# Every second up-projection weight pair: low part by an accumulating transfer instead of a VectorE subtraction

## The chip, the cores and the metric

The kernel runs on one core of one Trainium2 chip. The metric is the device time of one execution in microseconds (us). The time before is 1998.34 us, the median of two runs (1998.25 and 1998.43).

## The reference

One step of a hybrid encoder layer for 384 token rows (256 prompt frames and 8 streams of 16 frames), all in float32, with `D_MODEL` = 2048 and `D_FF` = 5632:

- `p = rmsnorm(x) @ w_in`, a convolution branch and an attention branch, and `x = x + (gate_a * a_out + gate_b * b_out) @ w_out` (the mixer);
- `up = rmsnorm(x) @ w_up`, with `w_up` of 2048 x 11264; the first 5632 columns go through a causal convolution of 3 taps and SiLU, the others multiply the result;
- `x = x + (silu(conv(g_half)) * u_half) @ w_down`, with `w_down` of 5632 x 2048.

The new keys, values, forget logits and convolution states are outputs as well. The change touches only how the weight tiles of `w_up` get ready for the matrix products.

## The kernel before, in words

**Three products for one.** The matmuls work on a rounded float32 format (`F32R`). To keep float32 accuracy, each operand is kept as a pair: `hi`, the rounded value, and `lo`, the rounded difference to the full value. A product is then three matmuls: activation hi by weight hi (line 251), activation hi by weight lo (L252), activation lo by weight hi (L253).

**Weight pairs.** Weights are streamed from memory once. The unit is a "pair": two blocks of 128 rows by 512 columns, one tile of 128 x 2 x 512 float32 (512 KB). The list `plan` holds all pairs in the order in which the products use them. `fetch` (L135 to L142) issues the load of one pair from SyncE's DMA queue (SP) into a tile `raw` (L140). `split_rows` makes `hi` by a ScalarE copy (L149) and `lo` by a VectorE subtraction `raw - hi` (L150). `raw`, `hi` and `lo` have three buffers each. So the `hi` and `lo` of pair n+3 can only be written when TensorE has finished with pair n, and the `raw` of pair n+3 can only be loaded when the last reader of `raw` of pair n has finished.

**Order.** `gemm` takes one pair for two steps of k. Before each pair it calls `ahead(3)`, which fetches and splits until three pairs are ready. The order of TensorE's instructions is that of the program (a manual schedule). Those of the other engines are placed by a scheduler when the program is built, with a priority for the splits (`SPLIT_AHEAD`); on the chip each engine works through its list strictly in order. The same holds for the DMA issues of SP and GpSimd (POOL).

**The feed-forward part.** `w_up` is used in 11 groups (g = 0 to 10) of 512 gate columns and 512 other columns. A group is two jobs of 8 pairs each: first the gate half, then the other half. Each pair feeds 18 matmuls (2 k steps, 3 token tiles, 3 products). After some groups the matching part of `w_down` is multiplied: the order is up 0 to 3, down, up 4 to 6, down, up 7 and 8, down, up 9 and 10, down.

**What else runs on the engines in a group.** At the end of each job ScalarE takes the three results out of PSUM (`up_evac`, L1003, tile `tok`). `turn` transposes them: three VectorE transposes into `tb` (L274), and 16 small SP transfers `uT<-tb` (L278). Behind the gate half, ScalarE copies the turned tile into `extf` (L1012), POOL fills in the borders (`L1018`, `L1019`) and copies the state out (`lc`, L1032), VectorE works the three taps (`gc`, L1027 and L1029), and ScalarE takes the SiLU (`sg`, L1031). Behind the other half, VectorE multiplies (L1058), ScalarE and VectorE split the product into hi and lo (`act`, L1060 and L1061).

Of the kernel before, what the change touches and what calls it, by code (L numbers as in the profile page):

```python
# [10 lines left out]
AF = mybir.ActivationFunctionType  # L11
ALU = mybir.AluOpType
# [29 lines left out]
def hybrid_step(  # L42
# [9 lines left out]
    nc = tc.nc  # L52
# [24 lines left out]
    def f(ap):  # L77
        return ap.bitcast(F32)
# [14 lines left out]
    def queued(d, chain=True):  # L93
        e = d.ins.engine
        if chain and e in newest:
            tc.add_manual_dep(d.ins, newest[e], mybir.DependencyInfo(
                mybir.DependencyClass.NoSync, mybir.DependencyReason.DATA), reason="queue")
        newest[e] = d.ins.name

    def load_x(c, n):  # L100
        cs = slice(c * P, (c + n) * P)
        o = c % 4 * P
        queued(nc.sync.dma_start(xs[c // 4][:, 0:2, o:o + n * P],
                                 x_prompt[0, :, cs].rearrange("(t p) d -> p t d", p=P)))
        queued(nc.sync.dma_start(xs[c // 4][:, 2, o:o + n * P], xin[2][:, cs]))
# [22 lines left out]
    def stream_tile():  # L128
        return rp.tile([P, 2, 512], F32, tag="raw", bufs=3, name="raw")
# [5 lines left out]
    def fetch(srcs):  # L135
        raw = stream_tile()
        o = 0
        for s in srcs:
            n = s.shape[-1]
            queued(nc.sync.dma_start(raw[:, :, o:o + n], s), len(plan) >= v_last)  # L140
            o += n
        return raw, o  # L142

    def split_tiles():
        return [wp.tile([P, 2, 512], F32R, tag=tag, bufs=3, name=tag) for tag in ("hi", "lo")]

    def split_rows(hi, lo, raw, o, k):
        first = in_first()
        queued(nc.scalar.copy(hi[:, k, :o], raw[:, k, :o]), first)  # L149
        queued(tt(lo[:, k, :o], raw[:, k, :o], f(hi[:, k, :o]), op=ALU.subtract), first)  # L150

    def split(raw, o):
        hi, lo = split_tiles()
        split_rows(hi, lo, raw, o, slice(0, 2))
        return hi, lo

    plan = []

    def planned(w, k0, cols, nk, *more):
        for k in range(k0, k0 + nk, 2):  # L160
            for cl in (cols,) + more:
                plan.append([w[0, k * P:(k + 2) * P, c:c + n].rearrange("(k p) n -> p k n", p=P) for c, n in cl])
# [11 lines left out]
    FFN_PLAN = [("up", g) for g in range(4)] + [("down", (0, 1, 2))]  # L174
# [12 lines left out]
    for what, g in FFN_PLAN:  # L187
# [3 lines left out]
        else:  # L191
            for cols in N_COLS:
                planned(w_down, 4 * g[0], cols, 4 * len(g))

    v_last = len(plan) - 16

    def in_first():
        return len(plan) >= v_last - 4
    ready = []
# [6 lines left out]
    def ahead(n):  # L206
        while plan and len(ready) < n:
            with tc.high_priority(offset=SPLIT_AHEAD):
                if x_left and (len(plan) - v_last) in range(3, 14, 2):
                    load_x(x_left.pop(0), 2)  # L210
                ready.append(split(*fetch(plan.pop(0))))

    def grouped(tiles):
        def get(k):
# [13 lines left out]
    def gemm(jobs, sides=(), wide=False):  # L228
        for js in jobs:
# [4 lines left out]
            for j, k in [(j, k + i) for k in range(0, js[0]["nk"], 2) for j in js for i in range(2)]:  # L234
                nb, n, nk, ps = len(j["ps"]), j["n"], j["nk"], j["ps"]
                kk = k % 2
                if kk == 0:
                    ahead(2 if len(plan) > v_last + 3 else 3)
                    hi, lo = ready.pop(0)
                ah, al = j["act"](k)  # L240
                st, sp = k == 0, k == nk - 1
                for m in range(nb):
                    s = slice(m * P, (m + 1) * P)
                    if j["kind"] == "A":
                        o = ps[m][:, :NT]
                        mm(o, hi[:, kk, s], ah, start=st, stop=False)  # L246
                        mm(o, hi[:, kk, s], al, start=False, stop=False)  # L247
                        mm(o, lo[:, kk, s], ah, start=False, stop=sp)  # L248
                    else:
                        o = ps[m][:, :n]  # L250
                        mm(o, ah[:, s], hi[:, kk, :n], start=st, stop=False)  # L251
                        mm(o, ah[:, s], lo[:, kk, :n], start=False, stop=False)  # L252
                        mm(o, al[:, s], hi[:, kk, :n], start=False, stop=sp)  # L253
                if sp:
                    with tc.high_priority(offset=EVAC_AHEAD):
                        for m in range(nb):
                            j["evac"](m, ps[m])
                    if "post" in j:
                        j["post"]()
                    if "done" in j:  # L260
                        j["done"]()
                tick(sides)
# [51 lines left out]
    with tc.manual_schedule(engines={ENG.SP, ENG.Activation, ENG.DVE}):  # L314
        nc.vector.memset(junk[:, 0:1], 0.0)
        nc.scalar.dma_start(gm_row[:], norm_mix_g[0].rearrange("(c p) -> c p", p=P))
        nc.scalar.activation(junk[:, 1:2], junk[:, 0:1], AF.Identity)
        load_x(0, 1)
        first = stream_tile()
        fetch_row(first, plan[0], 0)  # L320
        load_x(1, 1)
        fetch_row(first, plan.pop(0), 1)
        second = fetch(plan.pop(0))
        load_x(2, 2)
        warm = misc_tile()

        def warm_up(n):
            for _ in range(n):
                mm(warm[:, :P], ident[:], ident[:], start=True, stop=True)

        warm_up(WARM)
        pv = misc_tile()
        tr(pv[:, :16], gm_row[:], ident[:16, :16])
        nc.vector.tensor_copy(gm[:], pv[:, :16])
        hi, lo = split_tiles()
        split_rows(hi, lo, first, V_COLS[0][0][1], slice(0, 1))
        x_chunk(0)
        warm_up(FILL)
        split_rows(hi, lo, first, V_COLS[0][0][1], slice(1, 2))
        x_chunk(1)  # L340
        ready.append((hi, lo))
        ready.append(split(*second))
# [461 lines left out]
    for h in range(H):  # L804
        hi, lo = aHL[h // 4][:, 0, h % 4, :], aHL[h // 4][:, 1, h % 4, :]
# [326 lines left out]
```

## Time and profile before

| what | value |
|---|---|
| median of the runs shown | 1998.34 us |
| the profiled execution, its own time | 1997.35 us |
| its span (first to last instruction) | 1995.5 us |
| granted clock of TensorE in it | 0.999 |
| busy: TensorE / weight loads | 1986.3 / 1677.0 us |
| busy: VectorE / ScalarE / GpSimd | 1158.3 / 771.0 / 88.8 us |
| moved by DMA | 292.54 MB |

The profile comes from one profiled execution. Busy time is the time in which an engine's instructions ran; idle time has the instruction that ended it beside it, where the profile can tell. "L149" is line 149 of the kernel before. In the changed kernel the lines behind 151 stand 6 to 14 lines lower. In the timeline, each row has the start, the duration, the engine, the line and the operation; in brackets stands how long the engine had been idle and who ended that. SPq is SyncE's queue of DMA issues.

### The profile page before, as it was taken

The page shows a single profiled execution, that of the slowest core. Times are in us where ns is not written, and L with a number is a line of the kernel's source. Part 1 is how long each engine was busy: PE and PEld are TensorE (multiplying, and loading weights), DVE is VectorE, ACT ScalarE, POOL GpSimd, SP SyncE. Part 2 cuts the span into 40 slices and gives each one's busy share as a digit, 9 for nine tenths or more (in the row PEclk, how much of TensorE's full clock was granted, in tenths as well). Part 3 has the DMA queues.
Part 4 walks back from the last instruction along what each step waited for, and adds up shares of the span by engine and source line. Part 5 has one row for each costly group of instructions (what it writes and reads, how often), then busy time and mean ns, then how long its engine had stood idle before and what let it go on. Part 6 is the DMA issues. An engine that isn't in the chain of part 4 may idle for free.

```text
span 1995.5 us, 24829 instructions
## 1 busy us (share of the span) xinstructions
PE 1986.3 (100%) x9383; PEld 1677.0 (84%) x9383; DVE 1158.3 (58%) x1635; ACT 771.0 (39%) x1209; POOL 88.8 (4%) x216
## 2 busy tenths in 40 slices
PE   9999999999999999999999999999999999999999
PEld 9888999888888888888888888888888888888887
DVE  4455888888755487676455453345453345534563
ACT  5535454433334433344444442244342234323421
POOL 1000011000000000000100000000000000000000
PEclk9999999999999999999999999999999999999999
DMA  6564767444443435534555554445454445445543
GB/s 192 148 183 116 220 150 162 145 135 131 131 135 118 132 122 171 161 119 137 153 153 156 148 157 135 130 140 165 139 168 132 132 139 164 144 132 152 154 158 106
DMA packets 225384, 292.54 MB, mean 147 GB/s; under 512 B 61254, under 2 KB 112857, under 8 KB 225257
## 3 DMA queue, kind: packets, MB, share of 16 engines
q1 hardware_dynamic: 224945, 290.38, 49.7%
q8 instruction: 73, 1.20, 0.3%
q0 software_dynamic: 288, 0.57, 0.2%
q14 instruction: 46, 0.38, 0.1%
q10 hardware_dynamic: 32, 0.01, 0.0%
HBM read 266.98 MB, written 7.86 MB: 138 GB/s over the span
## 4 chain that ended last, share of the span: by engine, by line
PE 97%; DVE 2%; DMA 0%; issue 0%; SPq 0%; ACT 0%; DVEq 0%; ACTq 0%
PE acc L251 20%; PE acc L253 20%; PE acc L252 20%; PE misc L253 10%; PE misc L251 10%; PE misc L252 10%; PE acc L246 2%; PE acc L247 2%; PE acc L248 2%; DVE lo L150 0%; DVE mixT L268 0%; DMA bs<-c_dr 0%; PE misc L305 0%; PE misc L642 0%; PE misc L675 0%
## 5 line engine op out<-in xcount | busy, mean ns | idle before, releaser
L150 DVE TENSOR_TENSOR lo<-raw,hi 128x1024 fp32r<-128x1024 f32 (+2 forms) x481 | 580.3, 1207 | 676.3 <-ACT hi L149 674.1
L149 ACT CAST hi<-raw 128x1024 fp32r<-128x1024 f32 (+2 forms) x481 | 496.1, 1031 | 966.5 <-PE misc L253 781.1
L251 PE MATMUL acc<-hi,xg 128*128 128x512 f32 x704 | 275.1, 391 | 0.0
L253 PE MATMUL acc<-hi,xg 128*128 128x512 f32 x704 | 274.1, 389 | 0.0
L252 PE MATMUL acc<-lo,xg 128*128 128x512 f32 x704 | 274.1, 389 | 0.0
L251 PE MATMUL acc<-hi,hT 128*128 128x512 f32 (+1 forms) x512 | 193.4, 378 | 0.0
L253 PE MATMUL acc<-hi,hT 128*128 128x512 f32 (+1 forms) x512 | 190.7, 373 | 0.1
L252 PE MATMUL acc<-lo,hT 128*128 128x512 f32 (+1 forms) x512 | 190.7, 372 | 0.0
L251 PEld LDWEIGHTS acc<-hi,xg 128*128 128x128 f32 x704 | 132.2, 188 | 28.3
L253 PEld LDWEIGHTS acc<-hi,xg 128*128 128x128 f32 x704 | 132.2, 188 | 27.4
L766 DVE SCALAR_TENSOR_TENSOR ut<-ext,cw,ut 128x384 f32<-128x384 f32 x240 | 151.7, 632 | 6.0
L252 PEld LDWEIGHTS acc<-lo,xg 128*128 128x128 f32 x704 | 132.2, 188 | 27.0
L253 PE MATMUL misc<-hi,xg 128*128 128x512 f32 x352 | 137.1, 389 | 0.0
L251 PE MATMUL misc<-hi,xg 128*128 128x512 f32 x352 | 137.0, 389 | 0.0
L251 PE MATMUL acc<-hi,act 128*128 128x512 f32 x352 | 137.0, 389 | 0.0
L253 PE MATMUL acc<-hi,act 128*128 128x512 f32 x352 | 137.0, 389 | 0.0
L252 PE MATMUL misc<-lo,xg 128*128 128x512 f32 x352 | 137.0, 389 | 0.0
L252 PE MATMUL acc<-lo,act 128*128 128x512 f32 x352 | 137.0, 389 | 0.0
L253 PEld LDWEIGHTS acc<-hi,hT 128*128 128x128 f32 x512 | 96.4, 188 | 15.6 <-DVE hT L310 0.4
L252 PEld LDWEIGHTS acc<-lo,hT 128*128 128x128 f32 x512 | 96.5, 189 | 15.0 <-DVE lo L150 0.2
L251 PEld LDWEIGHTS acc<-hi,hT 128*128 128x128 f32 x512 | 96.5, 188 | 14.9 <-issue 0.2
L246 PE MATMUL acc<-hT,hi 128*128 128x384 f32 x256 | 89.4, 349 | 0.0
(326 smaller groups left out, 3034.9 us busy)
## 6 DMA issues: line engine op xcount, KB each, us to landing
raw<-in_w_up_dram SPq DMA_DIRECT2D x176, 512.0 KB
raw<-in_w_in_dram SPq DMA_DIRECT2D x96, 512.0 KB
raw<-in_w_down_dram SPq DMA_DIRECT2D x88, 512.0 KB
raw<-in_w_in_dram SPq DMA_DIRECT2D x64, 256.0 KB
raw<-in_w_out_dram SPq DMA_DIRECT2D x32, 512.0 KB
uT<-tb SPq DMA_DIRECT2D x336, 48.0 KB
raw<-in_w_att_out_dram SPq DMA_DIRECT2D x16, 512.0 KB
raw<-in_conv_pw_out_dram SPq DMA_DIRECT2D x16, 512.0 KB
```

Of the source, the lines that this page charges most:

```text
L149: queued(nc.scalar.copy(hi[:, k, :o], raw[:, k, :o]), first)
L150: queued(tt(lo[:, k, :o], raw[:, k, :o], f(hi[:, k, :o]), op=ALU.subtract), first)
L246: mm(o, hi[:, kk, s], ah, start=st, stop=False)
L247: mm(o, hi[:, kk, s], al, start=False, stop=False)
L248: mm(o, lo[:, kk, s], ah, start=False, stop=sp)
L251: mm(o, ah[:, s], hi[:, kk, :n], start=st, stop=False)
L252: mm(o, ah[:, s], lo[:, kk, :n], start=False, stop=False)
L253: mm(o, al[:, s], hi[:, kk, :n], start=False, stop=sp)
L766: stt(o, v, wc, o, op0=ALU.mult, op1=ALU.add)
```

## The change

In the up groups 1 to 9, every second pair (the 1st, 3rd, ... of the 16 pairs of a group) is split in another way. ScalarE makes `hi` as before; a second ScalarE instruction writes `-hi` into `lo`; then two transfers from the GpSimd queue, one for each 128 x 512 block, add the `raw` rows onto `lo` in place. The sum is again `raw - hi`, though the transfers write it as plain float32. The pairs in between, and all pairs of the other parts, are split as before. The set `summed` holds the positions of these pairs in `plan`, counted from its end.

```diff
-    def split(raw, o):
+    def split(raw, o, summed=False):
         hi, lo = split_tiles()
-        split_rows(hi, lo, raw, o, slice(0, 2))
+        if summed:
+            nc.scalar.copy(hi[:], raw[:])
+            nc.scalar.activation(lo[:], f(hi[:]), AF.Identity, scale=-1.0)
+            for k in range(2):
+                nc.gpsimd.dma_start(f(lo[:, k, :]), raw[:, k, :], accum_op=ALU.add)
+        else:
+            split_rows(hi, lo, raw, o, slice(0, 2))
         return hi, lo
...
+    summed = set()
+    left = len(plan)
+    for what, g in [("mixer", 0)] + FFN_PLAN:
+        n = {"mixer": left - sum(16 if w == "up" else 8 * len(g) for w, g in FFN_PLAN), "up": 16}.get(what) or 8 * len(g)
+        if what == "up" and 1 <= g <= 9:
+            summed |= set(range(left, left - n, -2))
+        left -= n
...
-                ready.append(split(*fetch(plan.pop(0))))
+                left = len(plan)
+                ready.append(split(*fetch(plan.pop(0)), left in summed))
```

## The prediction

> **What bounds the kernel now.** I read the page's totals and its chain first, then the groups of the two splitting lines, then the waits, and at last one up group in the timeline.
>
> ```profile
> span 1995.5 us, 24829 instructions
> PE 1986.3 (100%) x9383; PEld 1677.0 (84%) x9383; DVE 1158.3 (58%) x1635; ACT 771.0 (39%) x1209; POOL 88.8 (4%) x216
> ...
> PE 97%; DVE 2%; DMA 0%; issue 0%; SPq 0%; ACT 0%; DVEq 0%; ACTq 0%
> ...
> L150 DVE TENSOR_TENSOR lo<-raw,hi 128x1024 fp32r<-128x1024 f32 (+2 forms) x481 | 580.3, 1207 | 676.3 <-ACT hi L149 674.1
> L149 ACT CAST hi<-raw 128x1024 fp32r<-128x1024 f32 (+2 forms) x481 | 496.1, 1031 | 966.5 <-PE misc L253 781.1
> ```
>
> TensorE is busy for 1986.3 of 1995.5 us, and the chain that ended last runs through it for 97%. All the idle time that another change elsewhere could win back is 1995.5 - 1986.3 = 9.2 us, 0.5%. VectorE, which the change relieves, is idle for four tenths of the span, and ScalarE waits 781 us for TensorE to give back a `hi` buffer. The splits are early; the question is only whether they stay early enough. The room is read from the timeline of group g = 1, first TensorE's rows, then ScalarE's, then one of VectorE's:
>
> ```profile
> 977.90 0.39 PE L251 MATMUL acc<-hi,xg 128*128 128x512 f32 x1
> ...
> 981.98 0.39 PE L251 MATMUL acc<-hi,xg 128*128 128x512 f32 x1
> ...
> 994.22 0.39 PE L251 MATMUL acc<-hi,xg 128*128 128x512 f32 x1
> ...
> 1002.38 0.39 PE L251 MATMUL acc<-hi,xg 128*128 128x512 f32 x1
> ```
>
> ```profile
> 978.68 1.04 ACT L149 CAST hi<-raw 128x1024 fp32r<-128x1024 f32 x1
> 982.17 1.05 ACT L149 CAST hi<-raw 128x1024 fp32r<-128x1024 f32 x1 [2.46 <-PE misc L253]
> 986.25 1.05 ACT L149 CAST hi<-raw 128x1024 fp32r<-128x1024 f32 x1 [3.03 <-DMA uT<-tb]
> 993.31 1.05 ACT L149 CAST hi<-raw 128x1024 fp32r<-128x1024 f32 x1 [6.00 <-DMA raw<-in_w_up_dram]
> 996.11 0.98 ACT L1060 CAST act<-uT 128x384 fp32r<-128x384 f32 x2 [1.76 <-DMA raw<-in_w_up_dram]
> 997.00 1.05 ACT L149 CAST hi<-raw 128x1024 fp32r<-128x1024 f32 x1
> ...
> 1028.58 1.03 ACT L149 CAST hi<-raw 128x1024 fp32r<-128x1024 f32 x1
> ```
>
> ```profile
> 987.34 1.22 DVE L150 TENSOR_TENSOR lo<-raw,hi 128x1024 fp32r<-128x1024 f32 x1 [2.86 <-ACT hi L149]
> ```
>
> Pair 0 of the group starts on TensorE at 977.90, pair 1 at 981.98: 4.08 us for 18 matmuls, 0.23 us each. So pair 4 starts at 994.22, pair 6 at 1002.38, pair 14 at 977.90 + 14 x 4.08 = 1035.02. The copies listed are those of pairs 2, 3, 4, 5, 6 and (last) 14. Pair 4 is the clean case: its copy starts at 986.25, when TensorE has just freed the buffer, and its `lo` is first read by the second matmul, at 994.22 + 0.23 = 994.45. The **room** is 8.2 us, two pairs of matmuls. Before, `lo` is done at 987.34 + 1.22 = 988.56: 5.9 us to spare.
>
> **The change part by part.** Nine groups with eight pairs: 72 pairs, 144 transfers.
>
> *Removed:* 72 x 1.22 = 88 us of VectorE work, worth nothing: it lies beside TensorE. The 5.9 us to spare are late next.
>
> *Added, ScalarE:* a second pass over 128x1024, put at the 1.05 us of L149, the same shape; 76 us in all, hidden in ScalarE's 60% of idle time, but 1.05 us of each room. Two handovers cost about 0.04 us each (copy done at 987.30, VectorE starts at 987.34). From the copy's start to the first issue: 1.05 + 1.05 + 0.1 = 2.2 us.
>
> *Added, POOL and the transfers.* No accumulating transfer is in the trace. The nearest rows are the other transfers from POOL's queue (the issue; size and time to landing), one load of a pair on SP, and what the DMA engines carry (over the span: packets, MB, share; in groups 1 to 3, the last three columns: clock, DMA share, GB/s):
>
> ```profile
> L371 POOL DMA_DIRECT2D kg<-in_k_norm_g_dram x1 | 0.6, 569 | 0.0
> ```
>
> ```profile
> out_dram<-in_state_conv_dram POOLq DMA_DIRECT2D x1, 448.0 KB, 4.7
> ...
> kg<-in_k_norm_g_dram POOLq DMA_DIRECT2D x1, 64.0 KB, 5.5
> ...
> vrow<-in_norm_ffn_g_dram POOLq DMA_DIRECT2D x1, 8.0 KB, 2.4
> ```
>
> ```profile
> 979.56 9.38 SPq L278 DMA_DIRECT2D uT<-tb  x14
> 989.03 0.53 SPq L140 DMA_DIRECT2D raw<-in_w_up_dram  x1
> ```
>
> ```profile
> q1 hardware_dynamic: 224945, 290.38, 49.7%
> ```
>
> ```profile
> 977.90:1173.80 195.90, 195.90 (x867) 162.08 (x866) 99.52 (x127) 80.50 (x130) 11.94 (x36) 1.00 0.52 154
> ```
>
> An issue of 128 rows takes POOL 0.57 us; 144 of them are 82 us on an engine that is 4% busy. What counts is L, from the first issue to the landing of the second block. The floor is the 8 KB transfer's 2.4 us behind a second issue: 3.0 us. The ceiling is two transfers one behind the other at the 5.5 us of `kg`, 11 us. In between, the 448 KB transfer took 4.7 us, 2.3 more than the 8 KB one; for 512 KB that is 2.6 us. If the addition costs no more than a copy, L = 2.4 + 2.6 = 5.0. If its two operands, `raw` and `lo`, are read one behind the other, L = 2.4 + 2 x 2.6 = 7.6. I take 7.6: an addition has two operands to fetch, and the DMA engines are already 0.52 busy (154 GB/s) in these groups. D, from the copy's start to a ready `lo`, is then 2.2 + 7.6 = 9.8 us, against 8.2: **1.6 us too late** on a clean pair.
>
> The Trainium skill (DMA: Bandwidth & Descriptors, "Anatomy of one DMA — SWDGE (gpsimd) path") speaks for the change: it prices a GpSimd transfer at 2.0 us plus bytes over 436 GB/s, 2.6 us for one block, which would give an estimated L of 3.2 and no stall on a clean pair. By that rule the 448 KB transfer would take 3.1 us; the trace has 4.7.
>
> *How a stall adds up.* The copy of pair n+2 starts when TensorE has finished pair n-1, before a stall in front of pair n; so its room grows by that stall. Of two neighbouring summed pairs, the second is relieved. On some pairs the copy starts late already today: pair 2 at 978.68, 7.6 us ahead of 986.29, so 0.6 late (behind the `tok` copies); pair 6 at 997.00, 5.6 ahead of 1002.61, 2.6 late (its `raw` and the `act` work wait for the 14 small `uT` issues on SP), and in the changed order an `act` cast of 0.5 us plus handover stands between its two ScalarE passes, 0.6 more; pair 14 at 1028.58, 6.7 ahead of 1035.25, 1.5 late (behind `extf` and `sg`). This late work hangs on the end of the job, so stalls since then use it up. With 1.6 on top: pair 2, 2.2; pair 4, 1.6 - 2.2, nothing; pair 6, 1.6 + (2.6 - 2.2) + 0.6 = 2.6; pair 8, nothing; pair 10, like pair 2, 2.2; pair 12, nothing; pair 14, 1.6 (its 1.5 is used up by the 2.2); pair 0 of the next group, nothing. A group loses 8.6 us, nine lose **77 us**. Groups that follow a down block begin with a stall on pair 0 in place of part of pair 2's, with about the same sum.
>
> *Queued behind.* POOL's `extf` borders (L1018, L1019) and the state copies now share the in-order list with the transfers; POOL only waits there for ScalarE, which it waited for anyway:
>
> ```profile
> 1024.52 0.21 POOL L1018 COPY extf<-extf 128x30 f32<-128x30 f32 x1 [57.11 <-ACT extf L1012]
> ```
>
> The border block comes once a group, behind pair 12's transfers and ahead of pair 14's: bounds nothing and about 1 us a group (9 us in all); I take nothing, the taps being a pair earlier than their SiLU is needed. On SP, the load of pair n+3 now waits until the transfers of pair n have landed instead of for L150. A load takes 993.31 - 989.03 = 4.3 us, so it lands 9.8 + 4.3 = 14.1 us after pair n's copy; TensorE frees that buffer 13.9 us after it, and pair n+3 is a plain one with 5.9 us to spare: nothing. For pair 5 the issue stands at 989.03 behind the `uT` issues anyway; pair 2 lands at 978.68 + 9.8 = 988.5. If D passes 10.4 us, SP holds up the rest of the turn too.
>
> The sum against the profiled execution's own time, 1997.35 us (span 1995.5 and 1.85 around it), is 2074; against the median of the runs, 0.05% above it, **2075 us**. A change under 2% (40 us) is about what a measurement here can't tell from none.
>
> **The rivals.**
>
> *1. The transfers land in time (not slower).* One place decides: L of the two transfers. Below 5.9 us, D is at most 8.1 and the sum is pairs 2 and 10 0.5, pair 6 2.6, pair 14 0.9: 4.5 a group, 40 us. At L = 5.0, only pairs 6 (2.2) and 14 (0.5) stall: 2.7 a group, 24 us, 2022. At the floor of 3.0 it is about 2000. For it: the 4.7 us of 448 KB. Against it: this is one plain copy, alone, from one row. The Trainium skill's rule (DMA: Bandwidth & Descriptors, the section named above) belongs here, with an estimate of some 2002.
>
> *2. The adding is slow, or the DMA engines fill up.* They moved 290 MB in 49.7% of the span, 293 GB/s when busy. Two pairs take 8.16 us and carry 1 MB of loads; the added 512 KB, read twice, are another 1 MB, 128 GB/s on top of 154: 282 of 293. Queues then form, and L = 12 gives D = 14.2, 6.0 too late: pairs 2, 6, 10 6.6 each and pair 14 6.0, 25.8 a group, 232 us, 2230. Against it: counted once, the share would be 218 of 293. In this rival a stall is long enough for TensorE's clock to matter:
>
> ```profile
> 6.95 0.49 PE L253 MATMUL acc<-hi,hT 128*128 128x344 f32 x1
> 7.24 0.49 PE L251 MATMUL acc<-hi,hT 128*128 128x344 f32 x1
> ...
> 7.95 0.32 PE L251 MATMUL acc<-hi,hT 128*128 128x344 f32 x1
> 8.10 0.32 PE L252 MATMUL acc<-lo,hT 128*128 128x344 f32 x1
> ```
>
> At the kernel's start the matmuls stand 0.29 us apart, then 0.15: half rate at first. The Trainium skill (TensorE: Matmul & The Clock Gate, "Part 1: The HAM clock gate") says that an idle window of about 3.4 us sets the half rate again for as long; no stall in this trace is that long. By it, 36 stalls would add an estimated 36 x 1.7 = 61 us in rival 2, nothing in the forecast.
>
> *3. Faster.* Only the 9.2 us of idle TensorE time are there, and the build holds the 144 transfers and 72 fewer subtractions, so that the change isn't idle either.
>
> **How the numbers follow.** Forecast (L from 5.9 to about 10): 0.45. Rival 1: 0.27, all within 2%. Rival 2: 0.27. Rival 3: 0.01. So faster 0.01, within 2% 0.27, slower 0.72. Low end 2008 (L near 4, part of rival 1 left out), high end 2250 (L = 12 and some more; slower adders are left out).
>
> **What would show it.** Right: TensorE's idle time grows by some 77 us, in the groups 1 to 9 alone, in front of L252, ended by the transfer into `lo`; four stalls of about 2 us a group, in front of pairs 2, 6, 10, 14; L near 7.6; ScalarE busy 76 us more, VectorE 88 us less; `hi` copies waiting for TensorE less than 781 us. Wrong: L below 5.9; or above 10, with stalls on every other summed pair over 4 us and the DMA share near full; or loads of `raw` that land late and stall plain pairs, which I priced at nothing; or POOL's list holding up the taps.

## The result

The changed kernel takes **2065.63 us**, the median of its two runs (2062.57 and 2068.69), against 1998.34 us. The ratio is 1.034, with a 95% interval of 1.027 to 1.040: slower. The run that was profiled took 2068.69 us, 71.3 more than the profiled run before; its span grew by 71.5 us, from 1995.5 to 2067.0.

The page of the changed kernel, from the totals down to the issues:

```profile
span 2067.0 us, 25380 instructions
...
PE 2009.7 (97%) x9383; PEld 1682.5 (81%) x9383; DVE 1071.3 (52%) x1563; ACT 842.1 (41%) x1281; POOL 215.0 (10%) x360
...
q1 hardware_dynamic: 224945, 290.38, 45.2%
q0 software_dynamic: 21024, 38.33, 10.9%
...
PE 76%; DMA 8%; SPq 7%; DVE 4%; issue 2%; ACT 2%; POOL 1%; ACTq 0%; POOLq 0%; DVEq 0%
...
L150 DVE TENSOR_TENSOR lo<-raw,hi 128x1024 fp32r<-128x1024 f32 (+2 forms) x409 | 491.9, 1203 | 770.9 <-ACT hi L149 768.6
L149 ACT CAST hi<-raw 128x1024 fp32r<-128x1024 f32 (+2 forms) x409 | 420.5, 1028 | 860.1 <-PE misc L267 596.5
...
L158 POOL DMA_DIRECT2D lo<-raw x144 | 126.4, 1034 | 693.4 <-ACT lo L156 593.7
...
lo<-raw POOLq DMA_DIRECT2D x144, 256.0 KB, 4.2
```

VectorE gave up 87 us and ScalarE took on 71 us; neither is what the end hangs on. The `hi` copies of plain pairs now wait 596.5 us for TensorE, with the 85.0 of the summed ones (L155, another row of the groups) 681.5 instead of 781.1: they come later. TensorE's part of the chain fell from 97% to 76%, and the DMA transfers (8%) and SP's queue of issues (7%) came in, which had 0% before. TensorE does the same 9383 matmuls, but was idle for 2067.0 - 2009.7 = 57.3 us instead of 9.2, and busy for 23.4 us more. The added transfers have 10.9% of all DMA engine time for 38 MB, when the 290 MB of loads have 45.2%: 0.28% per MB against 0.16%.

What TensorE waited for (total us, times, longest):

```profile
PE acc L266 <- DMA lo<-raw: 30.1, 23, 3.2
PE misc L1050 <- POOL lc L1046: 14.3, 9, 2.3
```

The second row is a wait that was not there before: the transposes of the new state (L1050) stand between TensorE's matmuls and need `lc`, which POOL copies out of `extf` late. By place in the group, worked out from the start times of TensorE's rows (gaps above the usual 0.23 us, summed over the nine groups):

| where | us | predicted |
|---|---|---|
| in front of pair 6 (3.2 to 3.4 in each of six groups) | 19.7 | 23 |
| state transposes, in front of pair 13 (1.1 to 2.4 in each group) | 15.7 | 0 |
| matmuls at half rate behind stalls | 11.2 | 0 |
| pair 14 (0.5 to 1.2 in eight groups) | 5.5 | 14 |
| pair 0 | 5.0 | 0 |
| pair 5, a plain one | 4 | 0 |
| pair 2 | 3.0 | 20 |
| pair 10 | 0.4 | 20 |
| pairs 4, 8, 12 | 0 | 0 |

These are 64.5 of the 71.5 us. Comparing the start of every pair on TensorE with the trace before finds the rest: 1.2 us lie ahead of group 0, which the change doesn't touch, and 70.2 us in groups 1 to 9, at the same places (from the first matmul of pair 6 to that of pair 7 alone 31.8, half rate included). The three groups without a stall at pair 6 are 4, 7 and 9: they follow a `w_down` block, in which the product of the up group before has been split already.

**A clean pair is in time.** ScalarE's and POOL's rows for pair 12 of group 1, and TensorE's first readers of its two blocks, in the timeline of the changed kernel:

```profile
1026.25 1.05 ACT L155 CAST hi<-raw 128x1024 fp32r<-128x1024 f32 x1 [3.03 <-PE misc L267]
1027.34 1.06 ACT L156 ACTIVATE lo<-hi 128x1024 fp32r<-128x1024 f32 x1
```

```profile
1028.75 1.75 POOL L158 DMA_DIRECT2D lo<-raw  x2 [5.63 <-ACT lo L156]
```

```profile
1034.44 0.39 PE L266 MATMUL acc<-lo,xg 128*128 128x512 f32 x1
...
1036.48 0.39 PE L266 MATMUL acc<-lo,xg 128*128 128x512 f32 x1
```

The first issue comes 2.5 us after the copy's start. TensorE reads the first block at 1034.44, 5.7 us after that issue, and the second one nine matmuls later, at 1036.48, 7.2 us after its own issue (0.5 us behind the first). The tile view of `lo` for this pair gives the two times from issue to landing as least and greatest:

```profile
DMA to landing us min/median/max: 3.5/4.6/5.7
```

That leaves 2.2 and 1.5 us to spare, and TensorE doesn't wait. Over all 72 pairs the medians are 3.5 us from the first issue to the first block's landing and 5.5 us (4.7 to 9.8) from the first issue to the second's. From the start of ScalarE's copy that is 6.2 and 8.0 us.

**Pair 6 is late from several sides.** Pairs 5 and 6 of group 1, the group's first matmul and SP first, then ScalarE, POOL and TensorE:

```profile
979.13 0.39 PE L265 MATMUL acc<-hi,xg 128*128 128x512 f32 x1
```

```profile
980.79 11.15 SPq L292 DMA_DIRECT2D uT<-tb  x14
992.12 0.46 SPq L140 DMA_DIRECT2D raw<-in_w_up_dram  x1
```

```profile
998.35 1.05 ACT L149 CAST hi<-raw 128x1024 fp32r<-128x1024 f32 x1 [8.71 <-DMA raw<-in_w_up_dram]
...
1001.16 0.98 ACT L1074 CAST act<-uT 128x384 fp32r<-128x384 f32 x2 [1.76 <-DVE uT L1072]
1002.05 1.04 ACT L155 CAST hi<-raw 128x1024 fp32r<-128x1024 f32 x1
1003.00 0.51 ACT L1074 CAST act<-uT 128x384 fp32r<-128x384 f32 x1
1003.41 1.06 ACT L156 ACTIVATE lo<-hi 128x1024 fp32r<-128x1024 f32 x1
```

```profile
1004.83 1.74 POOL L158 DMA_DIRECT2D lo<-raw  x2 [13.14 <-PE misc L266]
```

```profile
1008.24 0.47 PE L266 MATMUL acc<-lo,xg 128*128 128x512 f32 x1 [3.11 <-DMA lo<-raw]
...
1009.05 0.63 PE L266 MATMUL acc<-lo,xg 128*128 128x512 f32 x1
1009.47 0.63 PE L267 MATMUL acc<-hi,xg 128*128 128x512 f32 x1
```

The 14 small `uT` issues take SP 11.15 us, 9.38 before. The load of pair 5 lands 998.35 - 992.12 = 6.2 us after its issue, 4.3 before. The group starts 1.2 us later than before (979.13 against 977.90); the `hi` of pair 5 starts 5.0 us later (998.35 against 993.31), the `act` work behind it too, and the `hi` of pair 6 at 1002.05 instead of 997.00. Against its group, pair 6 has lost 3.8 us. Its own transfer is quick (3.4 us from 1004.83 to 1008.24) and still too late. Behind the stall, from the third matmul or so on, the matmuls start 0.43 us apart: half rate, until about 1012, then 0.23 us again; the granted clock is 0.50 from 1008.9 to 1012.3. There are six such episodes of 6 to 13 matmuls, behind stalls of 3.27, 3.24, 3.40, 2.42, 3.27 and 3.25 us; the stall of 3.31 us brought none. The Trainium skill (TensorE: Matmul & The Clock Gate, "Part 1: The HAM clock gate") names an idle window of about 3.4 us; here stalls shorter than that were enough, and the measurement decides.

**In four of the six groups the turn itself starts late.** Group 1 shows slow issues and a slow load. In groups 2, 3, 5 and 8 the load of pair 5 takes 3.9 to 5.1 us (4.1 to 4.5 before), but it is issued 16.3 to 17.4 us after the group's start instead of 10.5 to 10.6. SP's wait around the start of group 2 (1052.82), its issues there, and the same place before, where the group starts at 1043.30:

```profile
SPq L140 <- DMA lo<-raw: 8.5, 1, 8.5
```

```profile
1056.29 0.89 SPq L140 DMA_DIRECT2D raw<-in_w_up_dram  x2
1057.24 12.82 SPq L292 DMA_DIRECT2D uT<-tb  x14
```

```profile
1044.96 8.79 SPq L278 DMA_DIRECT2D uT<-tb  x14
```

SP's next load needs the `raw` buffer of pair 0, whose two additions landed only 8.6 and 9.2 us after their issues, at 1056.15. SP works through its list in order, so the 14 issues of the turn stand behind that load: they begin 4.4 us after the group's start instead of 1.7, and take longer besides. In the four groups the second addition of pair 0 landed 10.8 to 12.3 us after ScalarE's copy began, in the other five 7.2 to 7.8 us. Why the additions of pair 0 were slow there stays open.

**The state transposes** wait in every group. Gate half of group 1, ScalarE's, POOL's and TensorE's rows:

```profile
1034.04 1.70 ACT L1026 COPY extf<-uT 128x128 f32<-128x128 f32 x8 [5.65 <-DMA uT<-tb]
1036.16 1.05 ACT L149 CAST hi<-raw 128x1024 fp32r<-128x1024 f32 x1 [0.42 <-DMA raw<-in_w_up_dram]
1037.12 0.90 ACT L1026 COPY extf<-uT 128x128 f32<-128x128 f32 x4
```

```profile
1037.47 1.20 POOL L1046 COPY lc<-extf 128x18 f32<-128x18 f32 x1 [1.01 <-ACT extf L1026]
...
1039.14 0.21 POOL L1046 COPY lc<-extf 128x18 f32<-128x18 f32 x1
```

```profile
1039.40 0.30 PE L1050 MATMUL misc<-ident,lc 128*72 128x128 f32 x1 [0.95 <-POOL lc L1046]
```

The same place before, from the timelines of ScalarE, POOL and TensorE:

```profile
1023.95 1.70 ACT L1012 COPY extf<-uT 128x128 f32<-128x128 f32 x8 [4.01 <-DMA uT<-tb]
```

```profile
1029.13 0.21 POOL L1032 COPY lc<-extf 128x18 f32<-128x18 f32 x1
```

```profile
1030.94 0.27 PE L1036 MATMUL misc<-ident,lc 128*72 128x128 f32 x1
```

Before, the gate job ended at 1010.54; the `extf` copies began 13.4 us later, the last `lc` was done at 1029.34, and TensorE came 1.6 us after it. Now the job ends at 1017.89, the copies begin 16.2 us later, and `lc` is done at 1039.35, when TensorE has already been waiting for it.

In group 1 and half of the next one the DMA engines were this busy (us of PE, PEld, DVE, ACT and POOL with their instructions, then the clock, the DMA share and GB/s):

```profile
977.90:1043.20 65.30, 60.48 (x258) 48.90 (x257) 21.43 (x32) 31.00 (x46) 16.10 (x26) 0.97 0.74 187
```

Before, groups 1 to 3 had a DMA share of 0.52 at 154 GB/s.

### The profile page after: what moved, and what is told of

Read it like the earlier page. It is cut to its first block, busy times and chain, and to the rows that moved or that the text cites. A ratio compares the mean times of both kernels' runs of the same rounds, so it can differ in the third digit from the quotient of the medians.

```text
span 2067.0 us, 25380 instructions
## 1 busy us (share of the span) xinstructions
PE 2009.7 (97%) x9383; PEld 1682.5 (81%) x9383; DVE 1071.3 (52%) x1563; ACT 842.1 (41%) x1281; POOL 215.0 (10%) x360
## 3 DMA queue, kind: packets, MB, share of 16 engines
q1 hardware_dynamic: 224945, 290.38, 45.2%
q0 software_dynamic: 21024, 38.33, 10.9%
## 4 chain that ended last, share of the span: by engine, by line
PE 76%; DMA 8%; SPq 7%; DVE 4%; issue 2%; ACT 2%; POOL 1%; ACTq 0%; POOLq 0%; DVEq 0%
PE acc L266 16%; PE acc L267 15%; PE acc L265 15%; PE misc L265 7%; PE misc L266 7%; PE misc L267 7%; SPq L292 7%; DMA lo<-raw 3%; PE acc L260 2%; PE acc L261 2%; PE acc L262 2%; DMA raw<-in_w_up_dram 2%; DMA uT<-tb 2%; DVE lo L150 1%; DVE tb L288 1%
## 5 line engine op out<-in xcount | busy, mean ns | idle before, releaser
L150 DVE TENSOR_TENSOR lo<-raw,hi 128x1024 fp32r<-128x1024 f32 (+2 forms) x409 | 491.9, 1203 | 770.9 <-ACT hi L149 768.6
L149 ACT CAST hi<-raw 128x1024 fp32r<-128x1024 f32 (+2 forms) x409 | 420.5, 1028 | 860.1 <-PE misc L267 596.5
L266 PE MATMUL acc<-lo,xg 128*128 128x512 f32 x704 | 281.2, 399 | 32.7 <-DMA lo<-raw 30.1
L265 PE MATMUL acc<-hi,xg 128*128 128x512 f32 x704 | 278.6, 396 | 0.0
L267 PE MATMUL acc<-hi,xg 128*128 128x512 f32 x704 | 277.9, 395 | 0.0
L158 POOL DMA_DIRECT2D lo<-raw x144 | 126.4, 1034 | 693.4 <-ACT lo L156 593.7
L265 PEld LDWEIGHTS acc<-hi,xg 128*128 128x128 f32 x704 | 134.5, 191 | 28.9 <-ACT hi L149 0.6
L267 PEld LDWEIGHTS acc<-hi,xg 128*128 128x128 f32 x704 | 134.8, 192 | 27.4
L155 ACT CAST hi<-raw 128x1024 fp32r<-128x1024 f32 x72 | 75.2, 1044 | 90.5 <-PE misc L267 85.0
L265 PEld LDWEIGHTS acc<-hi,hT 128*128 128x128 f32 x512 | 96.2, 188 | 16.3 <-ACT hT L323 1.4
L267 PEld LDWEIGHTS acc<-hi,hT 128*128 128x128 f32 x512 | 96.1, 188 | 16.2 <-DVE hT L324 1.0
```

The lines of the kernel that those rows point to most:

```text
L155: nc.scalar.copy(hi[:], raw[:])
L158: nc.gpsimd.dma_start(f(lo[:, k, :]), raw[:, k, :], accum_op=ALU.add)
```

## The experiments

Each starts from the changed kernel; its edit is shown against that. All ratios are to the kernel before, on the same chip. The changed kernel's own two runs lie 6 us apart, so a difference to its 2065.63 us is known to some 3 us.

| run | us | ratio, 95% interval |
|---|---|---|
| changed kernel | 2065.63 | 1.034 (1.027 to 1.040) |
| only_pair6 | 1998.78 | 1.0009 (1.0000 to 1.0019) |
| without_pair6 | 2036.16 | 1.0197 (1.0180 to 1.0213) |
| late_state | 2050.97 | 1.0271 (1.0256 to 1.0287) |
| plain_copy | 2001.72 | 1.0023 (1.0013 to 1.0032) |
| vector_add | 1996.80 | 0.9998 (0.9989 to 1.0008) |
| not6_late_state | 2034.46 | 1.0188 (1.0173 to 1.0203) |
| own_raw | 2042.07 | 1.0232 (1.0214 to 1.0249) |
| side_transfers | 2013.58 | 1.0078 (1.0061 to 1.0095) |
| without_pairs_2_4 | 2044.61 | 1.0235 (1.0220 to 1.0250) |
| odd_pairs | 2077.43 | 1.0403 (1.0387 to 1.0418) |
| one_transfer | 2076.50 | 1.0405 (1.0385 to 1.0425) |
| own_raw_not6 | 2016.72 | 1.0106 (1.0089 to 1.0122) |

The theories named in the expectations: **A**, clean pairs are in time, and the loss sits where ScalarE comes late (pair 6, the state transposes). **B**, the prediction's: every summed pair is late by a long L. In the later runs B stands for a narrower rival: pair 6 is late by its own second pass behind the `act` work. Three more concern what an addition does to its neighbours: **C** and **D**, it holds buffers, so that loads of `raw` come late; **E**, it fills the DMA engines and slows loads and turns.

### The second ScalarE pass alone: vector_add

```diff
-            for k in range(2):
-                nc.gpsimd.dma_start(f(lo[:, k, :]), raw[:, k, :], accum_op=ALU.add)
+            tt(lo[:], raw[:], f(lo[:]), op=ALU.add)
```

> The two transfers are replaced by a VectorE addition of raw onto lo; the second ScalarE pass stays. If the pass on ScalarE costs anything, it shows here. Theory A and rivals B and C alike: 5.9 us to spare less 1.1, so nothing: 1997 to 2000 us.

Measured: 1996.80 us, ratio 0.9998. The second pass and its handover cost nothing. All of the loss comes with the transfers.

### The transfer without the addition: plain_copy

```diff
-                nc.gpsimd.dma_start(f(lo[:, k, :]), raw[:, k, :], accum_op=ALU.add)
+                nc.gpsimd.dma_start(f(lo[:, k, :]), raw[:, k, :])
```

> The two transfers of a summed pair copy the raw rows onto lo instead of adding them (lo of these pairs is then raw itself, so the output is another one); same waits, same bytes written. Theory A: landing about 4 us after the issue as now, 2060 to 2068 us. Theory B: without the second operand L falls from 7.6 to 5.0 us and the time to 2022 us.

Measured: 2001.72 us; both theories had more, A because it took the 4 us landing for that of any transfer. Its page, the software queue and the group of the issues, and its tile `lo`:

```profile
q0 software_dynamic: 11808, 38.33, 5.1%
...
L158 POOL DMA_DIRECT2D lo<-raw x144 | 77.0, 539 | 688.2 <-ACT lo L156 673.6 <-ACT act L1074 10.6 <-issue 4.0
```

```profile
DMA to landing us min/median/max: 2.2/2.6/6.0
```

For the same bytes, an addition costs 2.2 times the engine time (10.9% of 2067.0 us against 5.1% of 1998.9), 21024 packets instead of 11808, 1034 ns of issue instead of 539, and 4.2 us to landing instead of 2.6. The same source, destination, queue, waits and held buffers without the add are nearly free: it is the adding. The Trainium skill's 2.6 us for 256 KB (DMA: Bandwidth & Descriptors, "Anatomy of one DMA — SWDGE (gpsimd) path") holds for this copy, and the time came out at the estimate of some 2002 us that went with it; it doesn't hold for the addition.

### One summed pair, or all but that one: only_pair6, without_pair6

```diff
-            summed |= set(range(left, left - n, -2))
+            summed.add(left - 6)
```

> Only pair 6 of each of the nine groups is summed (9 pairs in place of 72). Theory A (the transfers are in time on a clean pair; the loss sits where ScalarE comes late, on pair 6 above all, with the slow clock behind it, and in the state transposes that wait for GpSimd): pair 6 still stalls, by 1 to 2.5 us a group in the six groups that follow an up group, so 2008 to 2020 us; no stall in front of the state transposes. Theory B (as predicted: an addition lands 7.6 us after its issue and makes every summed pair 1.6 us late): pair 6 alone has no earlier stall to relieve it and loses 1.6 + 2.6 + 0.6 = 4.8 us in nine groups, 43 us, 2041 us.

Measured: 1998.78 us, below both theories; pair 6 stalls for 2.0 us in all. Waiting on the transfer, of all nine groups:

```profile
PE acc L266 <- DMA lo<-raw: 1.0, 3, 0.6
```

So the long way of pair 6 behind the `act` work is not late by itself. It takes the other additions.

```diff
-            summed |= set(range(left, left - n, -2))
+            summed |= set(left - j for j in range(0, n, 2) if j != 6)
```

> All summed pairs but pair 6 (63 pairs). Theory A: the 20 us of stalls on pair 6 and the 11 us of half-rate matmuls behind them go, 2030 to 2040 us; the state transposes still wait. Theory B: pairs 2, 8, 10, 12, 14 stall by 2.2, 1.6, 0.6, 1.0, 2.1 us, 7.5 a group, 68 us in all: 2066 us, no gain.

Measured: 2036.16 us, 29.5 less than the changed kernel. The stalls in front of pair 6 (19.7) and most of the half-rate time behind them (11.2, now 3.2) are gone: 27.7 us. The wait at the state transposes is unmoved:

```profile
PE misc L1050 <- POOL lc L1046: 16.7, 9, 3.1
```

### The state transposes later: late_state, not6_late_state

```diff
-            after(10, new_state)
+            after(16, new_state)
```

> The changed kernel, but the state transposes of a group come 16 steps of k behind the gate job in place of 10, three pairs later on TensorE. Theory A: the nine waits of TensorE for the copies into lc (15.7 us in the trace of the changed kernel) go, 2050 us. Theory B: nothing changes, 2066 us.

Measured: 2050.97 us, 14.7 less. The wait at the state transposes is gone, but not for nothing:

```profile
PE acc L266 <- DMA lo<-raw: 15.6, 17, 1.8
PE acc L266 <- DVE lo L150: 11.3, 15, 1.0
```

Pair 6 now stalls 6.4 us in all, pairs 13 and 14 14.2 and 16.1, pair 5 10.8. So the number came out near, by another sum than the theory's: a stall taken away in one place gave back room there and was met again at the next late pair.

not6_late_state has this edit and the one of without_pair6.

> Pair 6 split as before and the state transposes three pairs later, both together. If the two causes are separate, their gains add up: 2065.6 - 29 - 15 = 2021 us. If the one hides the other, more than 2030 us.

Measured: 2034.46 us, 1.7 us less than without_pair6, which is inside the spread of their runs. The two gains did not add: pair 14 stalls 15.3 us in all, pair 5 10.0 and pair 13 7.1. The state transposes hid a lateness of ScalarE and the transfers behind them; they were not a cost of their own.

### The DMA load alone: side_transfers

The pairs are split as before, and the two additions go from `hi` onto a tile that nobody reads. What is added is the load on the DMA engines and POOL, and that a transfer holds `hi`; no `lo` and no `raw` waits for it.

```diff
-            nc.scalar.copy(hi[:], raw[:])
-            nc.scalar.activation(lo[:], f(hi[:]), AF.Identity, scale=-1.0)
+            split_rows(hi, lo, raw, o, slice(0, 2))
+            if "side" not in res:
+                res["side"] = res["f"].tile([P, 2, 512], F32, name="side")
+                nc.gpsimd.memset(res["side"][:], 0.0)
+            side = res["side"]
             for k in range(2):
-                nc.gpsimd.dma_start(f(lo[:, k, :]), raw[:, k, :], accum_op=ALU.add)
+                nc.gpsimd.dma_start(side[:, k, :], f(hi[:, k, :]), accum_op=ALU.add)
```

> All pairs are split as before (ScalarE copy, VectorE subtraction); for the same 72 pairs two adding transfers of the same size run beside that, from hi onto a tile that nobody reads. No lo waits for a transfer and no raw is held. Theory A: the load alone makes the turn and the load of pair 5 late as in the changed kernel, so pairs 5 and 6 stall by about 1.4 us together in six groups, and GpSimd's list still delays the state transposes by up to 16 us: 2005 to 2025 us. Rival C (the waits do it: raw is held and lo comes late): 1997 to 2003 us.

Measured: 2013.58 us. TensorE's waits and the same window as above:

```profile
PE misc L1053 <- POOL lc L1049: 10.9, 9, 2.1
```

```profile
977.90:1043.20 65.30, 64.43 (x285) 52.93 (x284) 32.76 (x42) 26.03 (x42) 17.68 (x28) 1.00 0.85 209
```

The additions' load alone, in 0.85 of the DMA engines' time, brings the wait at the state transposes back (12.4 us by place, 15.7 in the changed kernel), and the `extf` copies start 16 to 17 us after the gate job's end, as there. It brings hardly any stall elsewhere (pair 5 1.0, and 1.7 inside pair 13, nearly all of it half rate). So the load makes the turn late, and this is about a quarter of the loss; the rest needs `lo` or `raw` to wait for the addition as well. The run isn't quite the load alone: ScalarE waited 31.2 us in all for a `hi` that a transfer held, and POOL 65.7 us for the addition before on the same tile, so the quarter is approximate.

### What makes pair 6 late: without_pairs_2_4

```diff
-            summed |= set(range(left, left - n, -2))
+            summed |= set(left - j for j in range(0, n, 2) if j not in (2, 4))
```

> Pairs 2 and 4 of each group are split as before; pairs 0, 6, 8, 10, 12, 14 stay summed (54 pairs). Theory A (the additions of pairs 2 and 4 load the DMA engines while the turn's small transfers and the load of pair 5 run, and that makes ScalarE late for pairs 5 and 6): pair 6 stalls no longer, although it is summed, and the half-rate matmuls behind it go; about 35 us less than the changed kernel, 2025 to 2035 us. Rival B (pair 6 is late by its own second ScalarE pass and its own additions, behind the act work): it stalls by 3 us in six groups as now, 2055 to 2066 us.

Measured: 2044.61 us, between the two ranges. Pair 6 stalls 6.0 us in all (0.6 to 1.6 in five groups) instead of 19.7; the state transposes 22.4, where the stalls of pair 6 no longer give them time:

```profile
PE misc L1050 <- POOL lc L1046: 21.0, 9, 3.5
```

The additions of pairs 2 and 4, which run while the product is turned and pair 5 is loaded, make two thirds of pair 6's stall. Whether by their load or by holding `raw` this run can't tell: the load of pair 5 needs the buffer of pair 2.

### Buffers of their own for raw: own_raw, own_raw_not6

The `raw` of a summed pair comes from two buffers of its own, so that a held `raw` doesn't keep a plain pair's load waiting. A scratch tile elsewhere shares a buffer to make space.

```diff
+        own = len(plan) + 1 in summed
-        raw = stream_tile()
+        raw = res["f"].tile([P, 2, 512], F32, tag="raw2", bufs=2, name="raw2") if own else stream_tile()
...
-            jk = res["f"].tile([P, 512], F32, tag="jk", bufs=1, name="jk2")
+            jk = res["f"].tile([P, NTT, 512], F32, tag="tok", bufs=1, name="jk2")[:, 0, :]
```

> The raw tiles of the summed pairs come from two buffers of their own in the feed-forward part's memory (a scratch tile of the mixer shares the tok buffer to make room), so that the three old raw buffers serve the plain pairs alone and the load of a plain pair never waits for an addition. Theory D (the raw buffer held until the additions have landed makes the loads of plain pairs late, and ScalarE, in order, late for the pair behind): the stalls on pairs 5 and 6 and their half-rate matmuls go, the waits of the state transposes stay: 2020 to 2035 us. Rival E (the additions slow the loads and the turn by filling the DMA engines, whoever holds a buffer): 2050 to 2066 us.

Measured: 2042.07 us, 23.6 less and outside both ranges: the held buffers cost something. But it went from other places than expected. The stall of plain pair 5 is gone (0.1 us) and the state transposes' (0.2); pair 6 still has 25.8 us, half rate included, and pair 14 has 11.1. Group 1 again, the turn's product on VectorE, then ScalarE:

```profile
994.65 1.03 DVE L1073 TENSOR_TENSOR uT<-uT,sg 128x384 f32<-128x384 f32 x2 [10.22 <-DMA uT<-tb]
```

```profile
995.24 0.98 ACT L1075 CAST act<-uT 128x384 fp32r<-128x384 f32 x2 [3.92 <-DVE uT L1073]
...
998.67 1.05 ACT L156 CAST hi<-raw 128x1024 fp32r<-128x1024 f32 x1
...
1029.58 2.50 ACT L1027 COPY extf<-uT 128x128 f32<-128x128 f32 x12 [3.18 <-DMA uT<-tb]
```

The load of pair 5 is early here, and the `act` work still waits, for the turn's transfers; the `hi` of pair 6 (998.67) stands behind it. And the wait at the state transposes went for another reason than buffers: the scheduler has put all twelve `extf` copies together (x12), where the changed kernel, like the kernel before, has a `hi` copy between the eighth and the ninth. So this run moves two things at once; that the buffers cost is shown for pair 5, not for the whole 23.6 us. Nor does it free SP: the loads of the summed pairs still wait for additions there, 252.8 us in all against 258.3, and in five groups the turn, whose issues stand behind them, still begins 2.6 to 4.3 us after the group's start.

own_raw_not6 has this edit and the one of without_pair6.

> own_raw, and pair 6 split as before (63 summed pairs with raw buffers of their own). If the loss that own_raw left is the stall of pair 6 (25.8 us in its trace, half-rate matmuls included) plus pairs 14, 0 and 2 (15.5 us), this takes the first away: 2012 to 2020 us. If freeing pair 6 only moves the stall to the next summed pair or to the state transposes: 2030 us or more.

Measured: 2016.72 us, 49 less than the changed kernel: these gains (23.6 and 29.5) nearly add. Most of what is left stands at pair 14 (12.5 us). It is the fastest of the variants that make `lo` by most of the additions, and still 20 us (2016.72 against 1996.41 for the kernel before in the same session) slower than before.

### The other pairs: odd_pairs

```diff
-            summed |= set(range(left, left - n, -2))
+            summed |= set(range(left - 1, left - n, -2))
```

> Pairs 1, 3, ... 15 of a group are summed in place of 0, 2, ... 14: the same number of transfers. If only the number counts: 2066 us. If the place decides, the late copies of pairs 5 and 13 (3 us each already before the change) now carry the long way and their pairs stall by 4 to 6 us in most groups, with the slow clock behind, while pair 6 is freed: 2080 to 2120 us.

Measured: 2077.43 us, just below the second range. Now pair 5 loses 26.8 us in all, pair 13 with the pair in front of it 50.0; some 18 us of this are half rate. But of the 50.0 us pair 13 itself has only 6.7. The rest is pair 12's, a plain one: in all nine groups TensorE waits for its `hi` (17.8 us) and then for its `lo`, because ScalarE copies it late, behind `extf` and a late load. The places are again those where `act`, `extf` and `sg` work or a late load hold up the copy; which of two neighbours is summed decides little.

### One transfer instead of two: one_transfer

```diff
-            for k in range(2):
-                nc.gpsimd.dma_start(f(lo[:, k, :]), raw[:, k, :], accum_op=ALU.add)
+            nc.gpsimd.dma_start(f(lo[:]), raw[:], accum_op=ALU.add)
```

> One adding transfer of 512 KB per summed pair in place of two of 256 KB. If GpSimd's second issue (0.9 us) counts in the room of a pair, up to 0.9 us less on each stalling pair and an eased list on GpSimd: 2045 to 2060 us. If the additions themselves fill the DMA engines: 2060 to 2068 us.

Measured: 2076.50 us, 10.9 more and above both ranges. The page's issue row:

```profile
lo<-raw POOLq DMA_DIRECT2D x72, 512.0 KB, 5.2
```

One addition of 512 KB lands in 5.2 us, about when the second of two does (5.5 us after the first issue), but 1.7 us later than the first of two (3.5). What is lost is that TensorE could begin with the first block: pair 6 now stalls 3.2 to 4.4 us in each of six groups, 35.3 in all with half rate, pair 14 15.4. So the block that decides is the first one.

## Why the prediction was right or wrong

The time was forecast within 10 us (2075 against 2065.63), and the loss of 77 us against 71.5. The sum hit, but not by its terms: the four places that it named (in front of pairs 2, 6, 10 and 14) have 28.6 us, and some 36 us came from places that it put at nothing. That the two errors cancel is luck.

**What bounds the kernel: right.** VectorE's 87 us were worth nothing, ScalarE's 71 us were hidden (vector_add, 0.9998), and no gain was to be had. The room of 8.2 us and the 2.2 us to the first issue hold (2.5 us in the rows shown).

**L, taken as 7.6 us: wrong; this is the term that was mis-sized.** The second block landed 5.5 us (median) after the first issue, nearer the single-read estimate of 5.0 that I set aside. The step that an addition costs as its two operands read one behind the other doesn't hold for the landing (4.2 against 2.6 us, 1.6 times), though it does for the engine time (2.2 times). I also measured D to the wrong event: TensorE needs the first block first, which was there 6.2 us after the copy's start, and the second 2.0 us later (one_transfer shows that this is worth 11 us). Against the second block's own room of 8.2 + 2.0 = 10.2 us even the forecast's D of 9.8 us was in time. So **"1.6 us too late on a clean pair" did not happen**: pairs 2 and 10 were forecast at 40 us together and cost 3.4. By its L the case was rival 1's, whose condition held and whose 2022 us did not, because it too counted only the summed pairs.

**Pair 6 as the worst place: right in place and size, incomplete in cause.** Forecast 2.6 us in each of nine groups, measured 3.25 in six. It was put down to today's lateness, the `act` cast between the passes and L; but only_pair6 shows that the first two are free alone (2.0 us in all), and without_pairs_2_4 that the additions of the two pairs before make two thirds of it. That it spares the groups behind a `w_down` block wasn't foreseen. Those groups were to begin with a stall on pair 0; they have none there, and four of the others do (5.0 us).

**"Nothing" for SP's loads, and for POOL's list and the taps: wrong, and the larger error.** The plain pair's 5.9 us to spare were counted against the held buffer, but not against a load that stands behind a late turn. The condition was on record (SP holds up the turn if D passes 10.4 us), but for pair 2; it was pair 0's D that passed it, with 10.8 to 12.3 us in four groups, and the `uT` issues took 10.5 to 13.1 us instead of 8.8 to 9.4 besides. The border block's bound of 9 us was for the taps; what came late was `lc`, which TensorE itself reads, with 1.6 us to spare before: 15.7 us. side_transfers shows that the load on the DMA engines brings this wait nearly by itself; own_raw, where the twelve `extf` copies stand together, has hardly any of it.

**"Nothing in the forecast" for the clock: wrong**, 11.2 us of half-rate matmuls. I left the term out by the window of about 3.4 us in the Trainium skill (TensorE: Matmul & The Clock Gate, "Part 1: The HAM clock gate"), which the stalls of 2.4 to 3.4 us here don't fill. The trace before had a case already, which I didn't read:

```profile
352.18 0.85 PE L642 MATMUL misc<-kTs,qz 128*32 128x128 f32 x16 [2.50 <-DVE kTs L623]
```

Behind this wait of 2.50 us the granted clock is 0.50 from 352.5 to 355.9, and matmuls of one shape stand 0.32 us apart instead of 0.17. The same wait of 2.50 us stands in all 14 traces; 5 have half rate behind it and 9 haven't. So a stall of the size that was forecast can bring half rate, but need not.

**Rival 2's mechanism was present in a small form**: the DMA share rose to 0.74, not to full, and what filled was not the additions' own queue but the turn's and the loads' time.

What stays open: how the loss at pairs 5, 13 and 14 divides between held buffers and loaded DMA engines (side_transfers has the load without a held `raw` and loses 16 us, own_raw less holding and gains 24, but with another order on ScalarE and with SP still waiting); and why some additions took 7 to 9 us. In plain_copy the load of pair 5 took as long in group 1 (6.4 us), and pair 6 stalled there too, by 1.7 us; but there the turn starts 1.7 to 2.1 us after the start of every group that has one. How the lateness moves when one stall is taken away (late_state) says that no place's share is a cost by itself.

## What to carry to other kernels

Moving work from an engine that has time to spare to the DMA queues wins nothing, and the price isn't the transfer's own landing alone: ask which small transfers and loads pass the same engines while it runs, and which of them has the least time to spare. Where a queue issues in order, a load that waits for a held buffer keeps everything behind it waiting too. Count room to the first byte that the consumer reads, with a semaphore for each part, and look beside the changed tiles for a reader on the critical engine that had a microsecond or two to spare. A stall of 2.5 to 3.4 us on TensorE should be priced with the chance of a half-rate stretch behind it, and a stall that is taken away with the next late pair that it had been hiding.

## What the hardware showed that was not expected

- An adding transfer of 256 KB from `raw` to `lo` took twice the issue time (1034 against 539 ns), 1.8 times the packets, 2.2 times the engine time and 1.6 times the landing time of a copy of the same size. In one piece, 512 KB landed in 5.2 us, against 3.5 for the first of two transfers of 256 KB.
- With these additions about, 14 of the small `uT` issues took SP's queue 10.5 to 13.1 us instead of 8.8 to 9.4. Without those of pairs 2 and 4 they took 8.8 to 9.9.
- Half rate followed most TensorE stalls of 3.2 to 3.4 us and one of 2.42 us. Behind one and the same wait of 2.50 us in the mixer it came in 5 of 14 traces. In the changed kernel's feed-forward part it lasted for 6 to 13 matmuls 0.43 us apart, with the granted clock at 0.50 for 3.4 us three times and for 6.8 us three times.
